# Loading the attention-output weights into slots earlier, and putting off the gate-weight differences, in a hybrid attention/HGRN2 block

## The chip, the cores and the metric

The kernel runs on one core of a Trainium2 chip. The metric is the device time of one execution in microseconds (us). The core has five engines with queues of their own: TensorE (PE; its weight loads are shown as PEld), VectorE (DVE), ScalarE (ACT), GpSimd (POOL) and SyncE (SP). Each engine works through its instructions in order. DMA transfers are issued by SP, ACT or POOL.

## The reference

A residual block over 1024 tokens with 1024 channels, all in float32. Two branches run on the same normalised input and are merged by gates, and an MLP follows.

```python
xn = rmsnorm(x, norm1_g)
u = xn @ w_in                      # q,k,v (512 each), f,i,q,g of HGRN2 (512 each), 2 x 1024 gates
o_sb = stick_breaking_attention(q_sb, k_sb, v_sb)         # 8 heads of 64
f = lb + (1 - lb) * sigmoid(f_raw); log_f = log(f)
k_hg = (1 - lb) * sigmoid(-f_raw)
o_hg = hgrn2_chunkwise(silu(q_hg), k_hg, i_hg, log_f)     # 4 heads of 128
o_hg = rmsnorm(o_hg, hg_norm_g) * silu(g_hg)
g_a, g_b = sigmoid(gate_sb + b[:1024]), sigmoid(gate_hg + b[1024:])
merged = g_a * (o_sb @ w_o_sb) + g_b * (o_hg @ w_o_hg)
h = x + merged @ w_out
h = h + square(relu(rmsnorm(h, norm2_g) @ w_ff1)) @ w_ff2
return rmsnorm(h, final_g)
```

## The kernel before

Every large product is done in split precision. `hi_lo` turns an f32 tile into a rounded part, with a cast on ACT (line 151), and a remainder, with a difference on DVE (line 156). `three` (matmuls on line 128) then multiplies high by high, low by high and high by low, so an operand is ready for PE only after its cast and its difference. Some of the products use sums and differences of blocks of the inputs and weights, as in a Strassen-like scheme, which costs DVE additions (line 1206) and differences (line 1209) and saves matmuls.

PE's program interleaves two lanes by hand. The *main* lane is the attention (`scores`, `weights`, `turn`, `values`), then the levels of the four HGRN heads (`hg_levels`, tiles `sl`, `sc`, `q`, `k`, `pp`) and their tails (`hg_tail`, tiles `pk`, `pkv`, `pho`, `pot`, `hon`). The *fill* lane is a `Stream` named `st`, a list of jobs. Each job is a projection with its weights; its body is a generator that yields after a few matmuls. `st.advance(n, upto)` runs `n` steps of it between two steps of the main lane. The table `FILL` says how many fill steps go with each main step for each HGRN head, and `upto` how far the stream may run.

The jobs of the stream are, in this order: `f_job(0)`, `q_job(0)`, `raw_job(8)`, `f_job(1)`, `q_job(1)`, `raw_job(9)`, `q_job(2)`, an `i` job, `f_job(2)`, `f_job(3)`, `q_job(3)`, then `raw_job(0)` to `raw_job(7)`, and `sb_job(0)` to `sb_job(3)`. A raw job is half of a merge gate's product: it uses two raw tiles `wga{n}r`, of which the second becomes a difference of both (`sub(rb, ra, rb)`, then one of its halves), then a cast and a remainder, tile `wga{n}t`. An `sb_job` multiplies the attention output (`asbh`, `asbl`, split from `osr`) with a quarter of `w_o_sb` (raw tile `wo0{n}r`, split to `wo0{n}h`, `wo0{n}l`) into the banks `pys`. After them come ten gate pairs (`GatePair`, raw tiles `wg{n}r`, splits `whig`, `wlog`, `tgh`, `tgl`) with products `gX` and `gY`.

When a job starts, `Stream._start` splits its weights and `prefetch` splits the next job's and loads those of the job after it. Jobs of class `RawUnit` are `late`: they prefetch inside their own body, after their first copy. Raw tiles come from a pool `wpool` with the tag `raw`, which has two buffers; `slot` takes one of the 40 tiles of a general pool. A unit's list `roomy` says which of its raw tiles are taken from slots instead of the pair. `after(ins, other)` holds an instruction behind another one in the scheduler's order.

`sum_forms` is a side generator of the `sb` jobs: one step of it runs with each fill step. It adds the low part onto the high part of the normalised input by accumulating DMAs on POOL (`whole_input`, line 1340, tiles `xnl`), then makes the sums `gs1` to `gs4` of quarters of it and their splits `gsh`, `gsl`, which `gX` and `gY` need. Near its end it loads the first gate pair's weights and the product sums that an earlier job stored to DRAM.

Of the kernel before, what the change touches and what calls it, by code (L numbers as in the profile page):

```python
# [23 lines left out]
KT = D // P  # L24
# [15 lines left out]
def kernel(  # L40
# [34 lines left out]
    def slot(name, dt=F32):  # L75
        return spool.tile([P, 1024], dt, tag="s", name=name)
# [19 lines left out]
    class Lane:  # L96
        def __init__(self):
            self.ends = []
            self.last = None
            self.gates = ()  # L100
# [4 lines left out]
    def after(ins, earlier):  # L105
        if earlier is not None and earlier.ins is not ins.ins:
            tc.add_manual_dep(ins.ins, earlier.ins.name, NOSYNC, reason="issue order")
        return ins

    def open_block(name):  # L110
        cur[0] = name
        lane = lanes[name]
        lane.gates = (lane.last,)
        if name == "main":
            lane.ends.append(lane.last)
        else:
            ends = lanes["main"].ends
            lane.gates += tuple(ends[-AHEAD : len(ends) - AHEAD + 1])
# [40 lines left out]
    def hi_lo(h, l, src):  # L159
        hi_copy(h, src)  # L160
        return lo_sub(l, src, h)
# [266 lines left out]
    class Unit:  # L428
# [5 lines left out]
        def split_t(self):  # L434
            pass
# [44 lines left out]
    class Stream:  # L480
        def __init__(self, eager=False):
            self.eager = eager
            self.jobs = []
            self.pos = 0
            self.gen = None

        def add(self, units, body):
            self.jobs.append((units, body))
            return len(self.jobs)
# [9 lines left out]
        def prefetch(self):  # L499
            nxt = []  # L500
            for us, _ in self.jobs[self.pos + 1 :]:
                nxt += [u for u in us if u.hl is None]
                if len(nxt) >= 2:
                    break
            if nxt:
                nxt[0].split()
                nxt[0].split_t()
            if len(nxt) > 1:
                nxt[1].load()

        def step(self):

            if self.gen is None:
                if self.pos >= len(self.jobs):
                    return False
                self._start()
            open_block("fill")
            if next(self.gen, StopIteration) is StopIteration:
                self.gen = None
                self.pos += 1  # L520
            return True
# [219 lines left out]
    lastsel, turn_lo = [None], [None]  # L741
# [133 lines left out]
    hg_sum, hg_level = [None], [None]  # L875
# [332 lines left out]
    def sub(out, a, b):  # L1208
        return nc.vector.tensor_tensor(out=out, in0=a, in1=b, op=ALU.subtract)
# [40 lines left out]
    class RawUnit(Unit):  # L1250
# [11 lines left out]
        def split(self):  # L1262
            if self.hl is not None:
                return
            self.load()
            ra, rb = self.raw
            h, l = (
                wpool.tile([P, 1024], F32R, tag=t, name=f"{self.name}{t}") for t in ("whi", "wlo")
            )
            hi_lo(h, l, ra)  # L1270
            sub(rb, ra, rb)
            sub(rb[:, 512:], rb[:, 512:], rb[:, 0:512])
            self.hl = [(h, l)]

        def split_t(self):
            if len(self.hl) == 1:
                t = slot(f"{self.name}t", F32R)
                self.hl.append((t[:, 0:512], t[:, 512:]))
                hi_lo(*self.hl[1], self.raw[1][:, 512:])
# [3 lines left out]
    def raw_job(cb):  # L1283
        u = raw_units[cb]

        def steps_of(ps, wt, w0, half_, k0, start):
            wh, wl = u.hl[wt]
            for k in range(4):
                c = (w0 + k) * P
                xh, xl = xn.mov(k0 + k, half_)  # L1290
                three(
                    ps, wh[:, c : c + P], wl[:, c : c + P], xh, xl, start and k == 0, k == 3, True
                )
                if k % 2 == 1:
                    yield

        def body():
            p1, p14, g1 = (half(f"{n}_{cb}") for n in ("p1", "p14", "g1"))
            ps, p4 = bank(f"pga{cb}"), bank(f"pgq{cb}")
            if 6 <= cb < KT:  # L1300
                load_g1(cb - 6)
            if 3 <= cb < KT - 1:
                osb[cb - 3] = slot(f"osr{cb}")
                load(osb[cb - 3], od[cb - 3])
            yield from steps_of(ps, 0, 0, 0, 0, True)
            hi_behind[0] = nc.scalar.copy(p1, ps)
            nc.scalar.dma_start(pd[cb][:, 0, :], p1)
            u.split_t()
            st.prefetch()
            hi_behind[0] = None  # L1310
            yield from steps_of(p4, 1, 0, 1, 4, True)
            add(p14, p1, p4)
            if cb == 3 or cb == KT - 1:
                whole_input(1, int(cb == KT - 1))
            nc.gpsimd.dma_start(pd[cb][:, 1, :], p14)
            yield from steps_of(ps, 0, 4, 0, 4, False)
            if cb < KT:
                nc.scalar.activation(g1, ps, AF.Sigmoid, bias=gate_bias(0, cb))
            else:
                nc.scalar.activation(g1, ps, AF.Sigmoid)  # L1320
                mul(g1, ps, g1)
            nc.scalar.dma_start(gd[cb], g1)
            if 4 <= cb < KT:
                a_sb.put(cb - 4, osb.pop(cb - 4))

        return st.add([u], body)

    side, g1r = [], {}

    def load_g1(cb):  # L1330
        g1r[cb] = half(f"g1r{cb}")
        load(g1r[cb], gd[cb])
# [10 lines left out]
    def sum_forms():  # L1343


        raw = whole
        def split(m, kp, src):
            forms[m, kp] = tuple(slot(f"gs{n}{m}{kp}", F32R) for n in "hl")
            hi_lo(*forms[m, kp], src)

        for j in range(2):
            whole_input(0, j)
        yield from range(WAIT)
        s1, s2 = {}, {}
        for kp in range(2):
            s1[kp] = slot(f"gs1{kp}")
            ins = add(s1[kp], raw[1, 0, kp], raw[1, 1, kp])
            if kp == 0:
                after(ins, hg_sum[0])
            yield  # L1360
        for kp in range(2):
            split(5, kp, s1[kp])
            yield
        for kp in range(2):
            s2[kp] = slot(f"gs2{kp}")
            sub(s2[kp], s1[kp], raw[0, 0, kp])
            yield
            split(6, kp, s2[kp])
            yield
        gates_in[0].load()  # L1370
        gates_in[0].load_sums()
        for kp in range(2):
            s3 = slot(f"gs3{kp}")
            sub(s3, raw[0, 0, kp], raw[1, 0, kp])
            yield
            split(7, kp, s3)
            yield
        for kp in range(2):
            s4 = slot(f"gs4{kp}")
            sub(s4, raw[0, 1, kp], s2[kp])  # L1380
            yield
            split(3, kp, s4)
            yield
        gates_in[0].split()
        gates_in[1].load()

    def sb_job(cp):
        src = W_OSB[:, cp * 256 : (cp + 1) * 256].rearrange("(k p) c -> p k c", p=P)
        unit = Unit(f"wo0{cp}", [[(0, 256, src)]])

        def body():
            if cp == 0:
                side.append(sum_forms())
            for j in range(2):
                cb = 2 * cp + j
                if 1 < cb + 1 < KT:
                    load_g1(cb + 1)
                g1 = g1r[cb]
                for i, cs in halves():
                    ps = bank(f"pys{cb}_{i}")  # L1400
                    for _ in proj_half(
                        ps, unit.hl[0], a_sb.mov, 4, i, lambda k: k * 256 + j * P
                    ):
                        next(side[0], None)
                        yield
                    if i == 0:
                        mul(g1, ps, g1)
                        nc.gpsimd.dma_start(yd[cb][:, i, :], g1)
                    else:
                        y = half(f"ys{cb}")  # L1410
                        nc.scalar.copy(y, ps)
                        nc.scalar.dma_start(yd[cb][:, i, :], y)

        return st.add([unit], body)
# [190 lines left out]
    gates_in = gp[KT:] + [gp[4 * i + j] for j in range(4) for i in range(2)]  # L1605
# [660 lines left out]
        values(*ready.popleft())  # L2266


    FILL = (3.4, 2.4, 2.8, 2.7, 2.9)
    owed = 0.0  # L2270
    for h in range(NHG + 1):
        lev = hg_levels(h) if h < NHG else iter(())
# [3 lines left out]
        while going:  # L2276
            going = False
            for g in (lev, tail):
# [3 lines left out]
                if next(g, StopIteration) is not StopIteration:  # L2282
                    going = True
                    owed += FILL[h]
                    st.advance(int(owed), upto)
# [105 lines left out]
```

## Time and profile before

| | us |
|---|---|
| runs | 1455.18, 1457.14, 1458.18 |
| median | 1457.14 |
| profiled execution | 1459.88 |
| its span, first to last instruction | 1458.1 |

The page of the profiled execution gives the busy time of each engine as a share of the span:

| engine | busy us | share |
|---|---|---|
| PE | 1431.9 | 98% |
| PEld | 1209.6 | 83% |
| DVE | 1119.4 | 77% |
| ACT | 675.1 | 46% |
| POOL | 145.6 | 10% |

A timeline row has the start and the duration in us, the engine, the line of the kernel, the operation, what it writes and reads, its shapes and the number of instructions put together; in square brackets stands the idle time of the engine before it and what ended that. A row of waits has the waiting engine, its tile and line, whom it waited for, and then the total, the number and the longest in us. A row of stretches has the window, its width, the busy time of PE, PEld, DVE, ACT and POOL with the instruction counts, the granted TensorE clock as a share of full speed, the share of the 16 DMA engines' time, and GB/s.

### The profile page before, as it was taken

To read this page: it belongs to the slowest core of one execution; us is meant where nothing else is said; L and a number is where in the kernel's file an instruction comes from. 1 tells how busy PE (TensorE), PEld (TensorE's weight loads), DVE (VectorE), ACT (ScalarE), POOL (GpSimd) and SP (SyncE) were. 2 spreads that over 40 slices of the span, in tenths; PEclk is the share of its full clock that TensorE was granted. 3 is DMA by queue.
4 is the path that set the end of the run, shared out by engine and by line. 5 is a ranking of instruction groups with operands and counts; after the bars stand their busy time and mean duration, and the time that the engine had idled before them with its cause. 6 is when DMAs were issued, how large, how long until landed. Compare 5 with 4: busy or idle time off the path is not lost.

```text
span 1458.1 us, 19537 instructions
## 1 busy us (share of the span) xinstructions
PE 1431.9 (98%) x7248; PEld 1209.6 (83%) x7248; DVE 1119.4 (77%) x1525; ACT 675.1 (46%) x1165; POOL 145.6 (10%) x338
## 2 busy tenths in 40 slices
PE   9999999999999998899999999999999999999998
PEld 8989988888888787788888888888888888888886
DVE  7799898988567786788777898666676757768765
ACT  7576675652143443333334575444444533533433
POOL 3121121200011032001000210000000000000032
PEclk9999999999999999999999999999999999999999
DMA  7234154442023694545478414444444975676825
GB/s 211 50 102 117 35 108 84 101 120 62 1 63 121 212 246 147 166 152 176 135 249 291 159 66 142 162 149 154 159 159 168 349 268 197 237 279 244 280 102 186
DMA packets 162359, 233.57 MB, mean 160 GB/s; under 512 B 26028, under 2 KB 95192, under 8 KB 162264
## 3 DMA queue, kind: packets, MB, share of 16 engines
q1 hardware_dynamic: 146424, 190.11, 38.5%
q0 software_dynamic: 11520, 34.61, 9.2%
q10 hardware_dynamic: 4320, 7.60, 1.4%
q8 instruction: 57, 0.93, 0.3%
q14 instruction: 38, 0.31, 0.1%
HBM read 167.27 MB, written 65.01 MB: 159 GB/s over the span
## 4 chain that ended last, share of the span: by engine, by line
PE 86%; DVE 6%; DMA 3%; issue 1%; ACT 1%; POOL 1%; SPq 0%; DVEq 0%; ACTq 0%; POOLq 0%
PE pm L128 21%; PE pX L128 9%; PE pW L128 6%; PE pY L128 6%; PE pjqk L128 6%; PE gX L128 4%; PE gY L128 4%; PE pyh L128 3%; PE po L128 3%; PE pji L128 3%; PE pjv L128 2%; PE pjq L128 2%; PE pwX L128 2%; PE z L128 2%; PE pjf L128 2%; PE pw L131 2%
## 5 line engine op out<-in xcount | busy, mean ns | idle before, releaser
L151 ACT CAST whid<-w 128x1024 fp32r<-128x1024 f32 x30 | 31.6, 1054 | 154.4 <-PE pm L128 86.1
L784 DVE TENSOR_TENSOR_SCAN rm<-rm,bits 128x511 f32<-128x511 f32 (+7 forms) x72 | 87.5, 1220 | 11.6 <-ACT rm L762 11.4
L128 PE MATMUL pm<-wlod,sh 128*128 128x512 f32 x240 | 93.5, 390 | 0.0
L128 PE MATMUL pm<-whid,sh 128*128 128x512 f32 x240 | 93.4, 389 | 0.0
L128 PE MATMUL pm<-whid,sl 128*128 128x512 f32 x240 | 93.4, 389 | 0.0
L128 PE MATMUL pm<-tl,sh 128*128 128x512 f32 (+1 forms) x210 | 81.3, 387 | 0.0
L128 PE MATMUL pm<-th,sl 128*128 128x512 f32 (+1 forms) x210 | 81.3, 387 | 0.0
L128 PE MATMUL pm<-th,sh 128*128 128x512 f32 (+1 forms) x210 | 81.3, 387 | 0.0
L156 DVE TENSOR_TENSOR wlod<-w,whid 128x1024 fp32r<-128x1024 f32 x30 | 36.7, 1223 | 56.4 <-ACT whid L151 56.4
L156 DVE TENSOR_TENSOR sl<-sa,sh 128x1024 fp32r<-128x1024 f32 x56 | 68.3, 1219 | 0.0
L151 ACT CAST wTh<-pw 128x512 fp32r<-128x512 f32 (+2 forms) x96 | 43.9, 483 | 47.3 <-PE pw L131 46.5
L2029 POOL TENSOR_SCALAR fss<-fss 128x1 f32<-128x1 f32 x8 | 4.5, 560 | 562.2 <-ACT fsc L2024 561.6
L151 ACT CAST sh<-sa 128x1024 fp32r<-128x1024 f32 x56 | 57.3, 1047 | 7.1 <-DMA sa<-ad 7.1
L156 DVE TENSOR_TENSOR wTl<-pw,wTh 128x512 fp32r<-128x512 f32 (+2 forms) x96 | 50.7, 548 | 3.8 <-ACT wTh L151 3.4
L128 PEld LDWEIGHTS pm<-wlod,sh 128*128 128x128 f32 x240 | 45.1, 188 | 9.7 <-DVE wlod L156 0.4
L128 PEld LDWEIGHTS pm<-whid,sh 128*128 128x128 f32 x240 | 45.1, 188 | 9.5
L128 PEld LDWEIGHTS pm<-whid,sl 128*128 128x128 f32 x240 | 45.0, 187 | 9.3
L164 DVE TENSOR_TENSOR bt<-bt,rm 128x511 f32<-128x511 f32 (+7 forms) x72 | 49.0, 686 | 3.7
L128 PE MATMUL pX<-sql,t1h 128*128 128x512 f32 x128 | 50.0, 391 | 0.1
L762 ACT ACTIVATE rm<-z 128x511 f32<-128x511 f32 (+4 forms) x96 | 48.0, 502 | 4.3 <-DVE g L164 1.3
L128 PE MATMUL pX<-sqh,t1l 128*128 128x512 f32 x128 | 49.8, 389 | 0.0
L128 PE MATMUL pX<-sqh,t1h 128*128 128x512 f32 x128 | 49.8, 389 | 0.0
(939 smaller groups left out, 4543.7 us busy)
## 6 DMA issues: line engine op xcount, KB each, us to landing
w<-in_w_ff_dram SPq DMA_DIRECT2D x72, 512.0 KB, 5.0
sa<-ad SPq DMA_DIRECT2D x56, 512.0 KB, 6.8
ad<-a SPq DMA_DIRECT2D x32, 256.0 KB, 2.0
ad<-s SPq DMA_DIRECT2D x16, 512.0 KB, 6.0
tw<-in_w_out_dram POOLq DMA_DIRECT2D x24, 256.0 KB, 4.0
pr<-pd SPq DMA_DIRECT2D x10, 512.0 KB, 5.8
x<-in_x_dram SPq DMA_DIRECT2D x8, 512.0 KB, 8.4
xnl<-xnh POOLq DMA_DIRECT2D x8, 512.0 KB, 10.1
```

The lines of the kernel that those rows point to most:

```text
L128: return pe(nc.tensor.matmul(*a, **k))
L131: return pe(nc.tensor.transpose(dst, src, ident))
L151: hi_last[0] = after(in_turn("act", nc.scalar.copy(dst, src)), hi_behind[0])
L156: nc.vector.tensor_tensor(out=dst, in0=src, in1=hi.bitcast(F32), op=ALU.subtract),
L164: return nc.vector.tensor_tensor(out=out, in0=a, in1=b, op=ALU.mult)
L762: nc.scalar.activation(rm[:, s0 + c0 - 1 : s0 + m - 1], z[:, c0:m], AF.Sigmoid, scale=-0.125)
L784: sc = nc.vector.tensor_tensor_scan(out=rr, data0=rr, data1=bits[:, 1024 - nk + a : 1024 - nk + b][:, ::-1], initial=rm[:, b : b + 1] if i ...
L2029: nc.gpsimd.tensor_scalar(out=ssq, in0=ssq, scalar1=1.0 / D, scalar2=EPS, op0=ALU.mult, op1=ALU.add)
```

## The change

There are five parts. (1) If the next job is a raw job and the current one isn't, `split_t` of the next job is not called at the start of the current job but at its sixth step, and its first difference is held behind the latest HGRN level's or turn's instruction. That concerns raw jobs 8, 9 and 0. (2) The two differences of the second raw tile move from `RawUnit.split` to `split_t`. (3) The raw tiles of the `sb` jobs come from slots, and the first three are loaded in raw jobs 5, 6 and 7. (4) In `sum_forms` the differences `gs3` and `gs4` and their splits lie in one step each, four yields fewer, and the first gate pair's split is moved ahead of `gs4`. (5) `FILL` has 2.2 instead of 2.4 for the second HGRN head and 2.9 instead of 2.7 for the fourth.

```diff
     class Stream:
+            self.steps = 0
+            self.owed_t = None
...
         def prefetch(self):
             if nxt:
                 nxt[0].split()
-                nxt[0].split_t()
+                if nxt[0].late and not self.jobs[self.pos][0][-1].late:
+                    self.owed_t = nxt[0]
+                else:
+                    nxt[0].split_t()
...
         def step(self):
             if self.gen is None:
+                self.steps = 0
                 self._start()
+            self.steps += 1
+            if self.owed_t and self.steps == 6:
+                self.owed_t.split_t(hg_level[0] or turn_lo[0])
+                self.owed_t = None
...
     class RawUnit(Unit):
         def split(self):
             hi_lo(h, l, ra)
-            sub(rb, ra, rb)
-            sub(rb[:, 512:], rb[:, 512:], rb[:, 0:512])
             self.hl = [(h, l)]

-        def split_t(self):
+        def split_t(self, behind=None):
             if len(self.hl) == 1:
+                ra, rb = self.raw
+                after(sub(rb, ra, rb), behind)
+                sub(rb[:, 512:], rb[:, 512:], rb[:, 0:512])
                 t = slot(f"{self.name}t", F32R)
...
     def raw_job(cb):
             if 6 <= cb < KT:
                 load_g1(cb - 6)
+            if 5 <= cb < KT:
+                sb_units[cb - 5].load()
             if 3 <= cb < KT - 1:
                 osb[cb - 3] = slot(f"osr{cb}")
...
     def sum_forms():
             sub(s3, raw[0, 0, kp], raw[1, 0, kp])
-            yield
             split(7, kp, s3)
             yield
+        gates_in[0].split()
         for kp in range(2):
             s4 = slot(f"gs4{kp}")
             sub(s4, raw[0, 1, kp], s2[kp])
-            yield
             split(3, kp, s4)
             yield
-        gates_in[0].split()
         gates_in[1].load()
+
+    sb_units = []
...
     def sb_job(cp):
         unit = Unit(f"wo0{cp}", [[(0, 256, src)]])
+        unit.roomy = (0,)
+        sb_units.append(unit)
...
-    FILL = (3.4, 2.4, 2.8, 2.7, 2.9)
+    FILL = (3.4, 2.2, 2.8, 2.9, 2.9)
```

## The prediction

> **What bounds the kernel now.** First the core's span and clock, then what TensorE (PE) waited for, over the whole span.
>
> ```profile
> core 0: 1458.1 us, clock 0.993
> PE sl L128 <- DVE q L164: 7.2, 3, 5.7
> PE gX L128 <- ACT whig L151: 4.1, 1, 4.1
> PE po L128 <- DVE wTl L156: 3.3, 2, 1.9
> PE gX L128 <- DVE gu L1206: 0.7, 1, 0.7
> PE gX L128 <- DVE wlog L156: 0.2, 1, 0.2
> ```
>
> Columns: total, times, longest. PE is the bound: these five are nearly all of its idle time after the start, so an edit gains only by closing one of them (or the slow clock behind it), and loses by opening one. The table by stretch says where they lie.
>
> ```profile
> 200.00:320.00 120.00, 116.67 (x650) 100.62 (x650) 107.07 (x155) 74.94 (x165) 22.70 (x77) 0.99 0.45 92
> 320.00:520.00 200.00, 199.28 (x1146) 168.45 (x1145) 148.65 (x227) 66.20 (x153) 13.37 (x19) 1.00 0.33 102
> 520.00:540.00 20.00, 20.00 (x116) 17.39 (x115) 13.94 (x21) 6.22 (x15) 8.00 (x10) 1.00 1.03 257
> 540.00:560.00 20.00, 13.02 (x89) 10.46 (x88) 18.57 (x25) 8.95 (x13) 1.67 (x3) 0.87 0.70 218
> 580.00:600.00 20.00, 15.67 (x60) 12.08 (x59) 14.74 (x18) 9.02 (x17) 3.68 (x3) 0.83 0.37 127
> ```
>
> Columns: width, busy time of PE, PEld, DVE, ACT, POOL, then the granted clock, DMA share, GB/s. The DMA engines are full in 520 to 540; PE idles in the next stretch while DVE is nearly full, and once more in 580 to 600. The timelines of SP, ACT and DVE give the cause of the long `sl` wait.
>
> ```profile
> 522.68 0.38 SPq L136 DMA_DIRECT2D wo01r<-in_w_o_sb_dram  x1
> DMA to landing us min/median/max: 16.0/16.0/16.0
> 538.75 1.05 ACT L151 CAST wo01h<-wo01r 128x1024 fp32r<-128x1024 f32 x1 [13.44 <-PE pys L128]
> 533.02 0.76 DVE L1103 COPY_PREDICATED sc<-masks,sl 128x512 f32<-128x512 uint8 x1
> 539.83 1.22 DVE L156 TENSOR_TENSOR wo01l<-wo01r,wo01h 128x1024 fp32r<-128x1024 f32 x1 [6.06 <-ACT wo01h L151]
> 540.98 2.35 DVE L1206 TENSOR_TENSOR gs<-xnl,xnl 128x1024 f32<-128x1024 f32 x2
> 545.07 0.68 DVE L164 TENSOR_TENSOR q<-q,pp 128x512 f32<-128x512 f32 x1
> 555.01 0.69 DVE L164 TENSOR_TENSOR q<-q,pp 128x512 f32<-128x512 f32 x1
> 545.90 1.17 PE L128 MATMUL sl<-q,k 128*32 128x32 f32 x32 [1.28 <-DVE q L164]
> 555.76 1.97 PE L128 MATMUL sl<-q,k 128*64 128x64 f32 x16 [5.70 <-DVE q L164]
> ```
>
> The 512 KB of `wo01r` took 16.0 us in the full stretch and landed at 522.68 + 16.0 = 538.7. ACT's cast began then (the PE that its row names was long done), and DVE stood 6.06 us at `wo01l` with the input sums `gs` and the last HGRN head's `q` queued behind. PE then waited twice for that `q`. The second gate wait has the same shape: `wg8r` is loaded only when the raw buffers of `wo02`/`wo03` come free, and its cast stands behind all the sums.
>
> ```profile
> SPq L136 <- DVE wo03l L156: 17.0, 1, 17.0
> 554.52 18.36 SPq L136 DMA_DIRECT2D wg8r<-in_w_in_dram  x3
> 588.61 1.04 ACT L151 CAST whig<-wg8r 128x1024 fp32r<-128x1024 f32 x1
> 589.70 0.80 PE L128 MATMUL gX<-gsh,whig 128*128 128x512 f32 x1 [4.10 <-ACT whig L151]
> ```
>
> The two `po` waits are in attention: DVE stands at a difference whose tile hasn't landed, with `wTl` behind it.
>
> ```profile
> 227.11 1.22 DVE L1209 TENSOR_TENSOR wga8r<-wga8r,wga8r 128x1024 f32<-128x1024 f32 x1 [2.56 <-DMA wga8r<-in_w_in_dram]
> 230.83 0.68 DVE L1209 TENSOR_TENSOR wga8r<-wga8r 128x512 f32<-128x512 f32 x1
> 279.38 1.22 DVE L1209 TENSOR_TENSOR wga9r<-wga9r,wga9r 128x1024 f32<-128x1024 f32 x1 [2.52 <-DMA wga9r<-in_w_in_dram]
> ```
>
> **The slow clock behind the gaps.** After the 5.70 and the 4.10 us gap the matmuls come at nearly half rate.
>
> ```profile
> 557.66 0.80 PE L128 MATMUL pys<-asbh,wo01h 128*128 128x512 f32 x1
> 561.66 0.41 PE L128 MATMUL pys<-asbh,wo01h 128*128 128x512 f32 x1
> 549.43 0.39 PE L128 MATMUL pys<-asbl,wo01h 128*128 128x512 f32 x1
> 549.66 0.39 PE L128 MATMUL pys<-asbh,wo01l 128*128 128x512 f32 x1
> 595.58 0.51 PE L128 MATMUL gY<-gsh,tgh 128*128 128x512 f32 x1
> ```
>
> At full rate starts are 549.66 − 549.43 = 0.23 apart. From 557.66 to 561.66 lie nine matmuls, 4.00 us for 2.07: 1.9 lost. From `gX` at 589.70 to `gY` at 595.58 lie twelve, 5.88 for 2.76; less the 0.2 wait, 2.9 lost. So 4.8 us in all, and it goes only if the gaps go. [...]
>
> **The change, part by part.** No instruction is added or removed: the same casts, differences, sums and loads stand in another order and in other buffers.
>
> *Differences of `wga8`, `wga9`, `wga0` later.* The two differences and the t split go to the sixth step of the job in front, on DVE behind a `turn_lo` or an HGRN level. Counted along the new order, DVE comes to them near 250 and 301; the tiles landed at 227.1 and 279.4, so DVE doesn't stop: −3.3 us of `po`. The moved work, 1.22 + 0.68 plus the t split, now lies in a stretch where DVE is busy 107.07 of 120 us. What hides it is the 12.9 us that DVE idles there, 5.1 of which were the two waits. A place without slack would return `po` waits: 0 to +3.3; I take +0.8, since the idle is four times the moved 3 us. For `wga0`, SP is touched too: its second raw buffer comes free later, so `wga1r`'s second load, in order on SP with `wga2r` behind it, goes out some 12 us later. The raw jobs have these rows:
>
> ```profile
> 478.35 1.23 DVE L1209 TENSOR_TENSOR wga4r<-wga4r,wga4r 128x1024 f32<-128x1024 f32 x1 [4.34 <-DMA wga4r<-in_w_in_dram]
> 472.04 0.99 SPq L136 DMA_DIRECT2D wga4r<-in_w_in_dram  x2
> 483.28 0.99 SPq L136 DMA_DIRECT2D wga5r<-in_w_in_dram  x2
> 493.60 2.11 SPq L136 DMA_DIRECT2D wga6r<-in_w_in_dram  x2
> ```
>
> A job lasts 10.3 to 11.2 us here (483.28 − 472.04, 493.60 − 483.28). Load, differences and splits take from 472.04 to 478.35, then 1.23 + 0.68 and two splits of up to 1.9, about 10: they fit, barely, so a delay at the head is caught up slowly but doesn't grow. 0 to +4; I take +0.5.
>
> *`wo00` to `wo02` into slots, loaded in raw jobs 5 to 7.* Three 512 KB loads move to a stretch with a DMA share of 0.33 out of one at 1.03. At 16.0 us a load they would still land 10 us before use. `wo01l` then waits for nothing but its buffer, and DVE comes to `gs` some 6 us sooner. That takes away the `sl` waits, 7.2, and the 1.9 of clock. What is late next: DVE's first sum needs an accumulated input half.
>
> ```profile
> L1340 POOL DMA_DIRECT2D xnl<-xnh x8: 867/896/1072, 432.5 to 532.1; - x8
> DMA to landing us min/median/max: 4.6/10.1/13.8
> ```
>
> The first sum reads the third of the last six (issued about 526), which at the median lands at 536; only that sum stands ahead of the next `q`, so `q` is ready near 539 for a PE that comes at about 544. The `q` after it has one more sum, three splits and a difference ahead (1.2 each, near 547) for a PE at 547 to 548: no stall, but no slack. New on ACT and DVE: the cast and difference of the last attention tile (`asbh3`, `asbl3`) now stand behind `wo01h`/`wo01l`, whose buffer PE frees with its last raw matmul, and PE's fourth step of the first output job waits for them: 0 to 2.3 (1.05 + 1.22); I take 1.2, as three steps of matmuls lie between.
>
> *Gate weights early.* `wg8r` no longer waits for `wo02`/`wo03` to free a buffer; its split goes ahead of the last two sums. `gX` then finds its weights: −4.1 − 0.2 and −2.9 of clock. The price: those four 1.2 us pieces of DVE work now mix with the last head's state updates and `hon`, with PE's `pho` and `pot` behind them: 0 to +4.9; I take +2.0, as DVE has about 10 us idle in 560 to 580 but not at the right places.
>
> *Yields and FILL.* Steps are only regrouped: ±0.5, taken as 0. The 0.7 at `gu` I leave.
>
> *Sum.* −3.3 − 7.2 − 1.9 − 4.1 − 0.2 − 2.9 = −19.6; +0.8 + 0.5 + 1.2 + 2.0 = +4.5; −15.1 us. The profiled execution took 1459.88 us (1.8 outside its span), so 1444.8; it is 2.7 above the median of 1457.14, which gives 1442.0.
>
> **The rivals.** What a measurement of this kernel can tell from no change is 0.2%, 2.9 us.
>
> 1. *The input sums stay bound by the accumulates.* With the loads gone the six transfers and the gate loads still fill the DMA engines (257 GB/s at 1.03); at the maximum of 13.8 us the first sum would start at 540, as before. Then `sl` keeps 7.2 and its 1.9: −6.0, 1451. Against it: half a megabyte has left that window, and only one sum is ahead of `q`. 0.11.
> 2. *The gate wait changes its name.* `gX` still needs the sums and PE the last head's results; if DVE's pieces delay `pho`/`pot` by about 5 us, 4.1 + 2.9 come back: −8.1, 1449. For it: DVE 18.57 of 20 in 540 to 560. 0.09.
> 3. *Both at once*: +1, 1458. 0.05.
> 4. *Slower: the raw jobs fall into step with their loads.* DVE already stands 4.34 us at `wga4r`, so the chain of about 10 us is near a job's 10.3. Started 12 us late, sharing SP and DMA with three more loads, it could be 3 us longer than a job in each of seven: +21 on −15.1 is +6, 1463. It decides from 2.6 us a job (18/7). Against it: a DMA share of 0.33, and that wait cost PE nothing. 0.10.
> 5. *The change doesn't do what it says in attention*: the later differences meet a full DVE, and `po` keeps its 3.3 us: −12.6, 1444.5. 0.08.
>
> **How the numbers follow.** The forecast has 0.57. Its own range is 1437 (all added terms at nothing, 1457.1 − 19.6) to about 1448 (twice the added terms and a half of case 2). The whole range, 1437 to 1453, takes in 1, 2 and 5 and leaves out 3 and 4. Faster: 0.57 + 0.11 + 0.09 + 0.08 = 0.85; same 0.05; slower 0.10.
>
> **What would show it.** Right: `wo01r` landed well before 520; DVE without idle before `wo01l`; no wait of PE on `q` above 2 us, none on `whig`; clock above 0.95 in every stretch from 520 to 600; the rows of `wga8r` and `wga9r` without a DMA wait. New: a wait of about 1 us at `pys` on `asbl`, and one at `pot`. Wrong: PE waits on `wga` tiles between 430 and 520 (case 4), on `q` with DVE stopped at `gs` on `xnl` (1), or on `hon` or `k` from 555 to 575 (2).

## The result, and the profile after

The changed kernel takes 1440.35 us (median of 4 runs, 1439.73 to 1441.67); the kernel before took 1456.81 in the same comparison. The ratio is 0.9889, with a 95% interval of 0.9871 to 0.9906: 16.2 us less (13.7 to 18.8). The forecast was 1442.0.

The two profiled executions differ by more, 1458.1 against 1438.7 us of span, because the one of before (1459.88) lies above the four runs of that comparison; a stretch of slow clock in it (last section) may be a part of why. First PE's waits in the changed kernel:

```profile
PE sl L128 <- DVE pp L164: 1.6, 2, 1.1
PE pga L128 <- DVE wga6wlo L156: 1.6, 1, 1.6
PE gX L128 <- DVE gu L1216: 0.7, 1, 0.7
PE po L128 <- DVE wTl L156: 0.5, 1, 0.5
PE z L128 <- DVE q L164: 0.2, 1, 0.2
```

The waits of 7.2 (`sl`), 4.1 (`gX` on `whig`) and 3.3 (`po`) are gone down to 1.6, 0 and 0.5. A new one of 1.6 stands at `wga6wlo`. The stretches of the changed kernel, with the same columns as before (width, busy time of PE, PEld, DVE, ACT, POOL, granted clock, DMA share, GB/s):

```profile
200.00:320.00 120.00, 119.33 (x673) 102.80 (x673) 111.55 (x161) 76.69 (x167) 22.76 (x77) 1.00 0.46 96
320.00:520.00 200.00, 197.90 (x1145) 167.96 (x1145) 147.65 (x227) 66.05 (x156) 12.82 (x20) 1.00 0.36 110
520.00:540.00 20.00, 20.00 (x108) 17.09 (x107) 16.86 (x24) 7.57 (x15) 8.37 (x10) 1.00 1.01 236
540.00:560.00 20.00, 18.90 (x131) 15.65 (x130) 18.60 (x27) 9.74 (x14) 1.64 (x3) 1.00 0.75 236
560.00:580.00 20.00, 20.00 (x108) 17.10 (x108) 18.29 (x25) 11.67 (x28) 4.66 (x6) 1.00 0.50 159
580.00:600.00 20.00, 20.00 (x89) 16.54 (x89) 13.81 (x21) 6.70 (x10) 1.08 (x2) 1.00 0.61 196
```

PE is busy 18.90 of 20 us in 540 to 560, where it had 13.02, and all the time in 580 to 600. The clock is 1.00 in every row, and the loss in 320 to 520 has grown from 0.7 to 2.1 us. DVE is now the engine near its limit from 540 to 580 (18.60 and 18.29 of 20). The timelines of SP, ACT, DVE and PE show the transfer, what has become late next, and the put-off differences:

```profile
507.44 0.37 SPq L136 DMA_DIRECT2D wo01r<-in_w_o_sb_dram  x1
527.68 1.05 ACT L151 CAST wo01h<-wo01r 128x1024 fp32r<-128x1024 f32 x1 [5.48 <-DMA g1r<-gd]
529.07 1.24 DVE L156 TENSOR_TENSOR wo01l<-wo01r,wo01h 128x1024 fp32r<-128x1024 f32 x1
530.87 1.23 DVE L156 TENSOR_TENSOR asbl<-osr,asbh 128x1024 fp32r<-128x1024 f32 x1 [0.56 <-ACT asbh L151]
535.32 1.22 DVE L1216 TENSOR_TENSOR gs<-xnl,xnl 128x1024 f32<-128x1024 f32 x1 [2.58 <-DMA xnl<-xnh]
545.58 1.12 PE L128 MATMUL sl<-q,k 128*64 128x64 f32 x16 [1.10 <-DVE pp L164]
573.82 0.48 PE L128 MATMUL gX<-gsh,whig 128*128 128x512 f32 x1
576.66 0.39 PE L128 MATMUL gY<-gsh,tgh 128*128 128x512 f32 x1
247.31 1.20 DVE L1219 TENSOR_TENSOR wga8r<-wga8r,wga8r 128x1024 f32<-128x1024 f32 x1
296.36 1.22 DVE L1219 TENSOR_TENSOR wga9r<-wga9r,wga9r 128x1024 f32<-128x1024 f32 x1
```

`wo01r` goes out at 507.4, where it went out at 522.7. DVE reaches `wo01l` at 529.1 without a wait, and then stands 2.58 us at the first input sum until its accumulate lands at 535.3. The first `gX` comes at 573.8 (589.7 before), and its twelve matmuls take 2.84 us (5.88 before). The differences of `wga8r` and `wga9r` come 20.2 and 17.0 us later than before and no longer wait for a DMA.

### The profile page after: what moved, and what is told of

Same layout as the page of the kernel before. It is cut to its first block, busy times and chain, and to the rows that moved or that the text cites. A ratio compares the mean times of both kernels' runs of the same rounds, so it can differ in the third digit from the quotient of the medians.

```text
span 1438.7 us, 19570 instructions
## 1 busy us (share of the span) xinstructions
PE 1424.3 (99%) x7248; PEld 1205.2 (84%) x7248; DVE 1118.1 (78%) x1525; ACT 675.7 (47%) x1165; POOL 139.5 (10%) x338
## 4 chain that ended last, share of the span: by engine, by line
PE 88%; DVE 5%; DMA 2%; issue 2%; ACT 1%; POOL 1%; SPq 0%; DVEq 0%; POOLq 0%; ACTq 0%
PE pm L128 21%; PE pX L128 9%; PE pW L128 6%; PE pY L128 6%; PE pjqk L128 6%; PE gX L128 4%; PE gY L128 4%; PE pji L128 3%; PE pyh L128 3%; PE pjf L128 3%; PE pjv L128 2%; PE po L128 2%; PE pjq L128 2%; PE pwX L128 2%; PE pys L128 2%; PE z L128 2%
```

## The experiments

All gains below are worked out from the ratio of a kernel's runs to those of the kernel before on the same chip, times 1457 us, with the 95% interval. Distances to the changed kernel are given by the medians and by these ratios, as the kernels ran in different comparisons. The diffs are shortened: dots and words stand for lines left out. The first four start from the kernel before and add one part each.

**One part alone: the deferral.**

```diff
+ if nxt[0].late and not self.jobs[self.pos][0][-1].late: self.owed_t = nxt[0]
+ ... split_t, with both differences, at the sixth step
```

> Before plus parts 1 and 2 alone (the differences of wga8, wga9 and wga0 put off). My theory: both po waits of 1.9 and 1.4 go, with the slow clock that the profile of before shows at 234 to 237 (about 1.5), and the waits at sl and gX stay as they are: about -4.5 us, 1452. Rival: the differences of wga0, put off, delay the raw jobs' weights, PE waits at wga6 for 1 to 3 us and the 7 us of sl waits grow or stay: -1 to -2 us.

Measured: 1456.77 us, ratio 0.9996 (0.9986 to 1.0006): 0.6 us less, with an interval from 2.0 less to 0.9 more. The waits of PE in its profile:

```profile
PE sl L128 <- DVE q L164: 8.2, 4, 5.7
PE gX L128 <- ACT whig L151: 3.6, 1, 3.6
PE pga L128 <- DVE wga6wlo L156: 0.6, 1, 0.6
PE po L128 <- DVE wTl L156: 0.4, 1, 0.4
PE pga L128 <- ACT p L1317: 0.4, 1, 0.4
```

The `po` waits went from 3.3 to 0.4 as they should. But `sl` has 1.0 more, `wga6wlo` 0.4 more and `p` 0.2 more: about half of it came back in the raw jobs and the HGRN levels beside them. The theory's −4.5 falls.

**One part alone: slots, without early loads.**

```diff
+ unit.roomy = (0,)
```

> Before plus slots for the raw tiles of the output weights, their loads still issued where the job in front prefetches them (no early loads). My theory: the landing in the full stretch of the DMA engines is the cause, so wo01r is still issued near 520, lands at 533 or later, and the sl waits keep at least 5 of 7.2 us: 0 to -3 us in all. Rival: the cause is the tie to the two raw buffers; then slots alone take away the sl waits and their slow clock and the gate weights come early: -8 to -12 us.

Measured: 1444.26 us, ratio 0.9915 (0.9901 to 0.9929): 12.4 us less (10.3 to 14.4). The theory's 0 to −3 falls; the rival is right, a little beyond its 8 to 12. In its profile, SP's timeline, the landing of `wo01r` and PE's waits:

```profile
517.41 0.38 SPq L136 DMA_DIRECT2D wo01r<-in_w_o_sb_dram  x1
542.76 5.50 SPq L136 DMA_DIRECT2D wg8r<-in_w_in_dram  x3
```

```profile
DMA to landing us min/median/max: 6.0/6.0/6.0
```

```profile
PE po L128 <- DVE wTl L156: 3.8, 2, 2.2
PE sl L128 <- DVE q L164: 2.7, 1, 2.7
PE gX L128 <- DVE wlog L156: 0.9, 1, 0.9
```

With a slot the prefetch doesn't wait for the raw pair. It goes out 5.3 us earlier, ahead of the six accumulates (the first is issued at 522.5) instead of among them, and lands in 6.0 us instead of 16.0. So the slow landing was the cause of the stop, and the tie to the two buffers was the cause of the slow landing. The same tie held `wg8r`: its three loads go out within 5.50 us from 542.8, where they took 18.36 from 554.5, and the waits at `gX` on `whig` and `wlog` fall from 4.3 to 0.9 although the split still stands behind all the sums. So slots alone removed most of both stops. Read off the two profiles, they took away 4.5 us of `sl` waits, 3.4 at `gX` and 5.7 of slow clock behind the two gaps (sized in the part on the prediction), and gave back 1.1 at `po`, `wga6wlo` and `gY`: 12.5, and the spans differ by 12.4.

**One part alone: slots and early loads.**

```diff
+ if 5 <= cb < KT: sb_units[cb - 5].load()
```

> Before plus part 3 whole (slots and early loads of wo00 to wo02), without the other parts. My theory: the sl waits go with their slow clock, -9 us; the gate weights' split is still behind all the sums, so PE's wait at gX for whig stays at 2 to 5 us: -8 to -10 us, 1447 to 1449. Rival: gX is bound by the sums' chain, which only starts with the accumulates; then its wait grows by what sl gave and the total is -1 to -3 us.

Measured: 1443.95 us, ratio 0.9914 (0.9901 to 0.9927), 12.5 us less: as with slots alone. The trace has 0.6 of `sl` wait left in place of 2.7, and `gX` waits 0.9; the expected 2 to 5 did not come, and the gain is larger than the expected 8 to 10.

**One part alone: the order of the sums and the gate pair's split.**

```diff
  for kp in range(2):  # gs3: sub, split, yield
+ gates_in[0].split()
  for kp in range(2):  # gs4: sub, split, yield
- gates_in[0].split()
```

> Before plus part 4 alone (four yields less, the first gate pair's split ahead of gs4). My theory: the gate weights still wait for the raw buffers and land near 576, so the split moved ahead makes DVE and ACT stand for them a little, but gX waits less than 4.1: 0 to -5 us. Rival: with the split ahead the last two sums come behind a late landing, and gX waits for these instead: 0 to +4 us.

Measured: 1452.21 us, ratio 0.9963 (0.9949 to 0.9976), 5.4 us less (3.5 to 7.4). The wait for `whig` is gone, and a smaller one at `hon` has come:

```profile
PE sl L128 <- DVE q L164: 5.9, 2, 5.7
PE po L128 <- DVE wTl L156: 3.8, 2, 2.3
PE pot L131 <- DVE hon L164: 1.9, 1, 1.9
```

The gains of the three separate parts add up to more than the whole (0.6 + 12.5 + 5.4 = 18.5 against 16.2). The 2.3 between them are within the intervals, but the traces show an overlap: slots and order each remove most of the wait at `gX`. The next five therefore take one part away from the changed kernel, or build up to it.

**Without the deferral.**

```diff
- if nxt[0].late and ...: self.owed_t = nxt[0]
+ nxt[0].split_t()          # differences back in split()
```

> The changed kernel without parts 1 and 2 (the differences of wga8, wga9, wga0 stand early again). By the prediction's terms: the po waits of 1.6 to 2.2 and 1.0 to 1.6 us return, raw jobs lose their small price: +2 to +4 us on 1440.4, 1442 to 1444. Rival, from the run of these parts alone, which moved the time by nothing that could be measured: 0 to +1 us.

Measured: 1441.91 us, ratio 0.9901 (0.9887 to 0.9915); 1.6 us behind the changed kernel by the medians and 1.7 by the ratios, with overlapping intervals. The `po` waits are back at 3.1, while `wga6wlo` is at 0.4 instead of 1.6: the same give and take.

**Without the new order of sums and split.**

```diff
- gates_in[0].split()       # ahead of gs4
+ gates_in[0].split()       # behind gs4, and four yields back
```

> The changed kernel without part 4 (four yields and the gate pair's split put back behind all sums). By the prediction's terms gX waits for whig again, 4 us and 2.9 of slow clock: +5 to +7 us, 1446. Rival, from the run of slots and loads alone, where gX waited only 0.9 us for wlog and gY 0.5: +1 to +2 us, 1442.

Measured: 1442.20 us, ratio 0.9904 (0.9889 to 0.9918): 1.9 us behind the changed kernel by the medians and 2.2 by the ratios, with overlapping intervals. PE's waits:

```profile
PE gX L128 <- DVE wlog L156: 1.1, 1, 1.1
PE gY L128 <- DVE pr L1216: 0.4, 1, 0.4
```

So with slots in place the order is worth about 2 us, not the 7.2 that stood at `gX` before.

**Slots, early loads and order, without deferral and new FILL.**

```diff
+ unit.roomy = (0,); early loads; gates_in[0].split() ahead of gs4
```

> Before plus slots, early loads and part 4 (no deferral, old FILL). If part 4 is worth what it gave against the changed kernel (1442.2 to 1440.4) it takes the 0.9 at gX and 0.5 at gY: -1 to -2 us on 1444.0, 1442 to 1443. Rival, the 5.2 us that it was worth alone: 1439.

Measured: 1442.43 us, ratio 0.9898 (0.9882 to 0.9913): 1.5 us less than without the order by the medians and 2.3 by the ratios (overlapping intervals), the waits at `gX` for `wlog` and at `gY` for `pr` gone from the trace, and `wga6wlo` up from 0.5 to 1.1. The part's 5.4 us alone is not an addition to the slots.

**Without the early loads.**

```diff
- if 5 <= cb < KT: sb_units[cb - 5].load()
```

> The changed kernel without the early loads (slots stay; wo00 to wo03 are loaded where the job in front prefetches them). By the run of slots alone, where wo01r went out at 517.4, ahead of the accumulates, and landed in 6.0 us: the early loads are worth 0 to 1 us, 1440 to 1441.5. By the prediction's text, which gave the gain to the move into raw jobs 5 to 7: wo01r is late again and sl waits 5 us or more, 1447 to 1450.

Measured: 1441.68 us, ratio 0.9894 (0.9875 to 0.9912): 1.3 us behind the changed kernel by the medians and 0.7 by the ratios, which can't be told from nothing. `wo01r` goes out at 510.3. Its profile has the waits of the changed kernel at the same places, 1.2 at `wga6wlo` and 1.2 at `sl`. That loading in raw jobs 5 to 7 makes the gain is refuted.

**With the old FILL.**

```diff
- FILL = (3.4, 2.2, 2.8, 2.9, 2.9)
+ FILL = (3.4, 2.4, 2.8, 2.7, 2.9)
```

> The changed kernel with the old FILL (2.4 for the second head, 2.7 for the fourth). The prediction counted FILL at 0: then 1440 +-1, with the 1.6 us wait at wga6wlo as it is. Rival: the new 2.2 is what brings PE to raw job 6 ahead of its weights or the old 2.7 is what brings the sl matmuls ahead of q: the wait at wga6wlo falls to 0.6 or less and the sl wait grows by 1 to 2 us.

Measured: 1441.01 us, ratio 0.9893 (0.9880 to 0.9907), no difference that can be told. PE's waits in it:

```profile
PE sl L128 <- DVE q L164: 2.4, 3, 1.5
PE pga L128 <- DVE wga6wlo L156: 1.3, 1, 1.3
PE sd L128 <- DVE sd_l L156: 0.5, 1, 0.5
PE pga L128 <- ACT p L1319: 0.4, 1, 0.4
```

The waits sit partly elsewhere (`sl` three times, `sd`, `p`): these rows sum to 4.6 us, where the changed kernel has 3.2 at `sl` and `wga6wlo`, without a difference in time that can be told. `wga6wlo` keeps 1.3, so the new FILL alone doesn't make it.

**With `wga0`'s differences early.**

```diff
- if nxt[0].late and ...:
+ if nxt[0].late and nxt[0].name != "wga0" and ...:
```

> The changed kernel with only wga0's differences early again (those of wga8 and wga9 stay put off). Theory: the late difference of wga0 delays wga1r's second load and through the pair of raw buffers all later loads, and makes the 1.6 us wait at wga6wlo: the wait falls to 0.5 or less, -1 to -1.5 us, 1439. Rival: that wait comes from the order of DVE's pieces or from FILL: the wait and the time stay, 1440 to 1441.

Measured: 1439.92 us, ratio 0.9887 (0.9873 to 0.9901), the lowest median of all, but not to be told from the changed kernel. The wait at `wga6wlo` falls only from 1.6 to 1.1 and the last `sl` wait grows from 1.1 to 1.7. The theory that `wga0` makes that wait does not hold.

**That kernel with the old fourth FILL value, and with the early loads a job later.**

```diff
+ FILL = (3.4, 2.2, 2.8, 2.7, 2.9)
+ if 6 <= cb < KT: sb_units[cb - 6].load()     # second kernel only
```

> The changed kernel with wga0's differences early and FILL (3.4, 2.2, 2.8, 2.7, 2.9): the new value for the second head, the old one for the fourth. With the old fourth value the kernel with both old values had no wait at the last sl matmuls (1.7 us in the run with wga0 early): -1 to -1.7 us, 1438 to 1439. Rival: q is bound by the accumulates' landing and the wait moves to another step of the last head: 1440.

> As the run with the fourth value of FILL old, but the early loads one raw job later (wo00 and wo01 in raw jobs 6 and 7, none in 5). If wo00r, issued right behind wga6r, is what makes wga6r land in 6.6 us and PE wait 1.1 to 1.6 us for wga6wlo, that wait falls to 0.5 or less: -0.6 to -1 us against its neighbour. Rival: wga6wlo is late by the order of DVE's pieces: no difference.

Measured: 1442.69 us (0.9898, 0.9880 to 0.9915) and 1443.24 us (0.9904, 0.9888 to 0.9920). Both are above the changed kernel, and the first is neither at the expected 1438 to 1439 nor at the rival's 1440. PE's waits in the first:

```profile
PE sl L128 <- DVE sc L1042: 1.6, 2, 1.3
PE sl L128 <- DVE pp L164: 0.7, 2, 0.5
PE pk L131 <- DVE k L164: 0.6, 1, 0.6
PE pho L128 <- DVE k L1152: 0.5, 1, 0.5
```

The wait at `wga6wlo` is gone in both, in the first with `wo00r` still right behind `wga6r`; so that load alone doesn't make it, and moving it gains nothing. The first differs from the kernel with `wga0` early, which waits 1.1 there, by the fourth FILL value alone; so that value has a part in this wait, though with all differences put off the wait stayed under the old FILL. The last head's waits are spread over `sl`, `pk` and `pho`: 3.4 us in these rows. The kernel with the new fourth value has 2.8 (1.1 at `wga6wlo` and 1.7 at `sl`). The 0.6 between them is less than the 1.6 us by their ratios, whose intervals overlap. The rest, and which of DVE's pieces sets `wga6wlo`, stay open. No version beat the changed kernel by more than its runs scatter.

## Why the prediction was right

**Direction and size.** The sum was −15.1 us, measured −16.2. The main cause was that the output weights' raw tiles were tied to the pair of buffers: `wo01r` then landed late and stopped DVE at `wo01l`, and `wg8r` came late to `gX`. Taking the tie away gave 12 of the 16 us, in the kernel with slots alone and again in the one with early loads too. That the number came so close is in part luck. The terms were read from a profiled execution of 1459.88 us and gave 1444.8 for it, and the profiled execution after took 1440.55, 4.3 less; going over to the medians hid most of that.

**The bill of the forecast, by its terms.** The waits in the trace after answer them:

| term | forecast, us | shown, us |
|---|---|---|
| `sl` waits | −7.2 | −5.6 (7.2 to 1.6) |
| slow clock after the gaps | −4.8 | −5.7, and 1.7 more in 234 to 238 (last section) |
| `gX` on `whig`, `wlog` | −4.3 | −4.3 |
| `po` waits | −3.3, +0.8 given back | −2.8 |
| raw jobs | +0.5 | +1.4 at `wga6wlo` (0.2 to 1.6) |
| `asbh`, `asbl` in front of PE | +1.2 | none in the list of waits |
| `pho`, `pot` behind the gate pieces | +2.0 | none: PE full, 20.00 of 20, from 560 to 600 |

The shown terms add up to −18.7 with the 1.7 counted, of the 19.4 us between the two spans. The slow clock was sized too small by 0.9: the sixteen `sl` matmuls right behind the gap of 5.70 us took 1.97 us before and take 1.12 now, and the prediction counted only from the `pys` matmuls behind them.

The costs were sized 4.5; the profile shows 1.4 in the raw jobs, 1.6 left at `sl` and 0.7 at `po` and `z`, 3.7 together. The two that were taken from bounds at DVE and ACT in the middle of the range, 1.2 and 2.0, didn't come, because DVE did those pieces while PE worked on what it had: ahead of `asbl` DVE stood only 0.56 us for ACT's `asbh`.

**The step that failed: which part makes the gain.** The prediction took slots and early loads as one part and put the 9.1 us of `sl` and its clock to the move of the loads into raw jobs 5 to 7. For the 7.2 us at `gX` it named the freed buffers and the split ahead of the last sums together. Slots alone gave 12.4, early loads added 0.1 to them, and taken from the whole they cost 0.7 to 1.3, which is within the noise. The order was worth 5.4 alone but about 2 with slots. That the loads had to leave the full stretch was right; a slot alone does that. The prediction read the tie to the raw pair, from `SPq` waiting 17.0 us for `wo03l`, but for `wg8r` only. The same list of the queue's waits in the kernel before, from 440 to 640, has it for the output weights too:

```profile
SPq L136 <- DVE wga7r L1209: 8.2, 1, 8.2
SPq L136 <- DVE wga7t L156: 2.5, 1, 2.5
```

`wo01r` could go out only when `wga7t`, the last reader of the raw tile it replaces, was done: that row's wait ends where the load starts, at 522.7. What looked like a place in the program's order was a wait for a buffer.

**Second, the deferral.** Its net was put at −2.0 (−3.3 + 0.8 + 0.5). Alone it moved the time by 0.6, between 2.0 less and 0.9 more; taken from the whole it cost 1.6 by the medians, which is not clear of the noise. The mechanism was right (3.3 to 0.4 in `po`), but the waits at raw jobs and HGRN levels grew by 1.6 in that profile, where the prediction gave back 1.3 in all. That PE now comes sooner to places where DVE's work doesn't would explain it; no run isolates this. `wga1r`'s second load, put at some 12 us later, goes out 3.1 later (426.5 before, 429.6 after).

**Third, the range.** Twice the added terms and a half of case 2 give −19.6 + 9.0 + 3.5 = −7.1, so the forecast's own range ends at 1450 and not at 1448. The result doesn't hang on it.

**The signs and the rivals.** The signs of being right came: no wait on `whig`, none on `q` above 2 us, the clock at 1.00 from 520 to 600, `wga8r` and `wga9r` without a DMA wait. The waits expected at `asbl` and `pot` did not. The rival with the accumulates as the bound has a foot in the trace: DVE stands 2.58 us for `xnl` at the first sum, and PE 1.10 at `sl`. The `sl` waits that are left are 1.6, not 9.1 with their clock; only one sum stands ahead of the next `q`. The gate wait didn't change its name with the whole change. With the order alone it did, 4.1 becoming 1.9 at `hon`. The raw jobs did not fall into step with their loads: 1.6 us at one tile. Attention did as the change says.

## What to carry to other kernels

When a load is late, look first at what held its issue. Here `wo01r`, in a pool of two buffers, went out at 522.7, when the last reader of the older tile was done, and not when the program asked for it. With a buffer of its own it went out at 517.4, ahead of a burst of other transfers, and landed in 6.0 us instead of 16.0; slots alone were worth 12.4 us, the new order alone 5.4. Gains of parts that remove the same wait don't add (the order was worth 5.4 alone and about 2 with slots in place), so cost each part once with the others in place and once alone. And where a wait is closed, look at the next places for what comes back: with the deferral alone the waits at `po` fell by 2.9 us and those at `sl`, `wga6wlo` and `p` grew by 1.6.

## What the runs showed of the hardware

The prediction counted the slow clock behind the gaps of 5.70 and 4.10 us. The traces say more exactly where it lies. In the kernel before, the granted clock is 0.50 from 234.01 to 237.42, from 554.86 to 561.69 and from 589.00 to 595.82, and 1.00 between these. The first stretch is 3.41 us long and the other two 6.83, twice as much; the starts lie 320.85 and 34.14 us apart, 94 and 10 times 3.413. From 200 to 600 us the traces of the fourteen kernels have eight such stretches: these three, two with the deferral alone, two with the order alone and one with slots alone. The other ten kernels are at 1.00 there. Rows in steps of 3.41 us, laid so that the changes of the clock fall on their ends, follow for the kernel before (around the gaps of 1.91 and 5.70 us), for slots alone (2.71) and for the order alone (2.25 and 1.89). PE's busy time, as the profile counts it, is the second number, the granted clock the third from the end:

```profile
230.60:234.01 3.41, 1.50 (x13) 1.39 (x12) 3.41 (x7) 0.37 (x1) 0.00 (x0) 1.00 0.00 0
234.01:237.42 3.41, 3.41 (x14) 3.12 (x13) 2.63 (x5) 1.79 (x5) 1.26 (x4) 0.50 0.20 8
551.45:554.86 3.41, 0.00 (x0) 0.00 (x0) 3.41 (x4) 2.61 (x5) 0.00 (x0) 1.00 0.41 154
554.86:558.28 3.42, 2.52 (x18) 2.31 (x19) 3.19 (x6) 0.52 (x1) 0.45 (x1) 0.50 0.52 153
558.28:561.69 3.41, 3.41 (x10) 2.64 (x9) 1.04 (x4) 0.06 (x1) 0.09 (x1) 0.50 0.20 77
```

```profile
547.75:551.16 3.41, 1.63 (x8) 1.00 (x6) 2.29 (x3) 2.64 (x4) 0.46 (x1) 1.00 1.00 281
551.16:554.58 3.42, 2.49 (x22) 2.21 (x23) 3.42 (x7) 1.04 (x3) 0.42 (x1) 1.00 0.82 270
```

```profile
228.95:232.37 3.42, 1.92 (x10) 1.38 (x9) 3.42 (x6) 0.37 (x1) 0.00 (x0) 1.00 0.02 5
232.37:235.78 3.41, 2.65 (x20) 2.66 (x21) 3.31 (x6) 0.53 (x2) 0.00 (x0) 1.00 0.00 0
580.53:583.94 3.41, 1.52 (x9) 1.03 (x8) 2.51 (x4) 1.53 (x2) 1.87 (x1) 1.00 1.03 322
583.94:587.35 3.41, 3.41 (x9) 2.65 (x8) 2.71 (x3) 1.26 (x2) 0.61 (x1) 0.50 0.90 312
```

In these rows 1.50, 0.00 and 1.52 us of PE's work are followed by a step at half clock; 1.63, 2.49, 1.92 and 2.65 us are not. At half clock the step with 2.52 us of work is followed by another one, and the three that PE fills (from 234.01, 558.28 and 583.94) by full clock. That is what was measured: no run changes PE's work in one such step alone, so that it is this work that decides, and where a limit would lie, was not shown.

The length of a gap alone doesn't say whether it counts. From 200 to 600 us, half clock followed all five gaps of 3.6 us or more: 5.70 and 4.10 in the kernel before, 5.7 and 3.6 with the deferral alone, 5.7 with the order alone. It followed none of 1.8 us or less. Of the five between, it followed those of 1.89 (order alone), 1.91 (before) and 2.17 us (slots alone); it did not follow those of 2.25 (order alone) and 2.71 us (slots alone), although they are longer. In the rows above, the gaps of 1.89 and 1.91 us lie inside one step, and those of 2.25 and 2.71 us are divided between two. The slow stretch at 234.01 begins 1.4 us behind the gap that ended at 232.63. Half clock lasted about 3.4 us behind the three short gaps and about 6.8 behind the five long ones.

The prediction did not count the stretch at 234.01, which cost half of its 3.41 us, 1.7. In these traces a gap of about 2 us thus cost an estimated 1.7 us or nothing. The runs of one kernel differ too: that with the order alone ran from 1448.61 us at a mean granted clock of 0.998 to 1454.18 at 0.994. The stretches themselves are seen in the profiled executions only.
